# A causal convolution of 31 taps on four engines: the low parts of nine weights by an adding transfer, more taps on GpSimd, TensorE's taps in two chunks

## The chip, the cores and the metric

The kernel runs on one core of a Trainium2 chip. A core has five engines that work side by side, each through its own queue of instructions in a fixed order: TensorE (PE in the profile; PEld is its loading of weights), VectorE (DVE), ScalarE (ACT), GpSimd (POOL) and SyncE (SP), which here only starts transfers. Engines wait for each other through semaphores. The metric is the device time of one execution in microseconds (us). Before the change the median of three runs is 1430.38 us, from 1429.72 to 1431.05.

## The reference

The program is a decoder trunk of two layers over 512 positions of width 1024, in float32. Each layer has a token mixer, a cross-attention into 256 memory tokens and a gated MLP. The change lies in the mixer of the second layer:

```python
def conformer_conv(x, norm, w1, b1, dw_w, dw_b, ln_g, ln_b, w2, b2):
    h = rms_norm(x, norm) @ w1 + b1
    h = jax.nn.glu(h, axis=-1)               # first half times sigmoid(second half)
    h = causal_dwconv(h, dw_w, dw_b)         # 31 taps along the positions, one weight per channel
    h = jax.nn.silu(layer_norm(h, ln_g, ln_b))
    return h @ w2 + b2
...
    m = rms_norm(mem, mem_norm)              # cross-attention, right behind it
    k = (m @ wk).reshape(Bn, M, XA_HEADS, XA_HD)
    v = (m @ wv).reshape(Bn, M, XA_HEADS, XA_HD)
```

The keys and values of the cross-attention depend on the memory alone, so their products can be done at any time before.

## The kernel before

Activations are held transposed: channels on the 128 partitions, in eight chunks of 128, and the 512 positions along the free dimension. TensorE multiplies in a rounded float32 format, so each operand is split into a high part (a rounded copy, made by ScalarE) and a low part (operand minus high part, a subtraction on VectorE or GpSimd). One product of float32 accuracy is then three matmuls (`mm3`, lines 184 to 188): high by high, high by low, low by high. A 128 x 1024 weight has eight 128 x 128 blocks, so one projection onto a chunk (`project`) is 24 matmuls over 512 positions. A key piece (`Memory.products`) is 24 matmuls over 256 memory tokens.

In the conformer (line 1398 on) chunk c goes through these steps. Two projections give its halves, G (the gate) and V. `sigmoid(c)` on ScalarE turns G into the gate; `gated(c)` on VectorE (L1413) multiplies V by it and gives the convolution's input h. The 31 taps of a chunk are shared out:

- `PE_GROUPS[c]` groups of four taps go to TensorE (`conv_pe`, L1443). For them `gated` has GpSimd zero four leading columns of h (L1412) and SyncE start four transfers that stack shifted copies of h (L1420); `taps_of` has GpSimd build the table of tap weights (L1433). A group is four small matmuls, eight records in the profile.
- `N_POOL[c]` taps are set aside (`set_aside`): ScalarE scales a shifted h (L1465, L1468), and GpSimd adds it to a sum (L1469), all but the first.
- The rest are on VectorE (`conv`, L1478 and L1480): one multiply-add each into a bank of PSUM. Two auxiliary banks serve these sums.

`merge(c)` (L1484, VectorE) adds the two sums and the bias. Then follow the sums over channels for the LayerNorm, `quarters` (L298, TensorE): the first half takes chunks 0 to 3, the second half all the rest. TensorE fills the time of the LayerNorm with the products of the memory's values (`Memory.sums`, L458).

Weights stream through three raw buffers and four pairs of high and low buffers. `fetch` starts the transfer of a weight; `weights` splits one that has come. The order is G0, V0, G1, V1, ... G7, V7, then the keys' weights K4 to K7, then the values' R0 to R7. A pair of buffers is given back by the projection that used it, so the split of a weight waits for the projection four places before. The first four splits have their subtraction on VectorE, the later ones on GpSimd (L167 in the profile, as all splits). The weights of keys 0 to 3 have been split and parked by the stage before. Keys 0 and 1 are made before the conformer's projections, key 2 around the first of them.

From the first projection to the last merge the order on all five queues is written out by hand, as a script of steps: G, V project; g is the sigmoid, S the gated product (with the zeroing and the stacking transfers), T a tap on VectorE, P a tap set aside, M a merge, F a fetch and a split, C TensorE's taps, W their table, K a key's products, k and l its high and low part, Q the first half of the channel sums. Each step puts its instructions on its engines' queues, and no queue passes over one that waits. Ahead of the script, where the tokens' scales are computed, a scheduler orders the instructions by priority.

Of the kernel before, what the change touches and what calls it, by code (L numbers as in the profile page):

```python
# [15 lines left out]
P = 128  # L16
# [17 lines left out]
C_RG = 8.0  # L34
TAPS = 31

PE_GROUPS = [0, 0, 0, 4, 0, 0, 4, 6]
N_POOL = [6] * 7 + [5]

KE = 2  # L40
PARKED = 4
# [20 lines left out]
def trunk(ctx: ExitStack, tc: tile.TileContext, I: dict, out: list):  # L62
# [16 lines left out]
    def nm(s):  # L79
        uid[0] += 1  # L80
        return f"{s}_{uid[0]}"
# [1316 lines left out]
    def conformer(norm, nxt, mem, parked):  # L1398
        fold = small.tile([P, 32], F32, tag="fold", name="fold", bufs=1)
        V.tensor_reduce(fold, ident.rearrange("p (a b) -> p a b", b=4), axis=mybir.AxisListType.X, op=ALU.add)  # L1400
        hs, outs = [None] * C, []

        b, psa = [None] * C, [None] * C

# [77 lines left out]

        def merge(c):
            V.scalar_tensor_tensor(zs[c], accs[c], col("c_dw_b", c), zs[c], op0=ALU.add, op1=ALU.add)  # L1484
            outs.append(zs[c])

        def warm(name, func, ins):
            with tc.issue_after(ins):
# [2 lines left out]
        taps, accs, zs, aside, convs = [[None] * C for _ in range(5)]  # L1491
        names = [k + str(c) for c in range(C) for k in "GV"]
        names += ["K%d" % n for n in range(PARKED, C)] + ["R%d" % n for n in range(READY)]
        raws, ws = [], {}

        def fetch():
            if len(raws) < len(names):
                k, n = names[len(raws)][0], int(names[len(raws)][1:])
                src = I["pw1"][n + (C if k == "G" else 0)] if k in "GV" else I["wk" if k == "K" else "wv"][mem.layer * C + n]
                raws.append(wp.tile([P, D], F32, tag="raw", name=nm("raw"), bufs=3))  # L1500
                Memory.fetched = nc.sync.dma_start(raws[-1], src)

        def weights(eng=None):
            k = names[len(ws)]
            ws[k] = load_w(raw=raws[len(ws)], eng=eng, park=k in ("R0", "R1", "R2", "R3"))

        for _ in range(4):
            fetch()
# [3 lines left out]
        warm("token", AF.Sqrt, norm.square)  # L1512
        for n in range(KE):
            mem.keys(n, parked[n])
            if n == 1:
                with tc.high_priority(URGENT):
                    norm.scale()
# [8 lines left out]
        xs = [None] * C  # L1526
        mem.eng = G
        with tc.manual_schedule(engines=ORDERED | {mybir.EngineType.SP}):
            key2 = mem.products(parked[2], ks=range(4))
            ps0 = project_all([ws["G0"], ws["V0"]], norm.x[:1], last=False)  # L1530
            mem.products(parked[2], key2, range(4, C))
            project_all([ws["G0"], ws["V0"]], norm.x[1:], ps0, 1)
            mu = stat_ps()

            def run(script):
                for step in script.split():
                    k, c, n = step[0], int(step[1:2] or 0), int(step[2:] or 1)
                    if k in "GV":
                        raw[step] = project(ws[step], c, norm.x)
                    elif k == "g":  # L1540
                        sigmoid(c, raw["G%d" % c])
                    elif k == "S":
                        psa[c] = raw["V%d" % c]
                        gated(c)
                    elif k == "T":
                        convs[c] = convs[c] or conv(c)
                        for _ in range(n):
                            next(convs[c])
                    elif k == "P":
                        for _ in range(n):  # L1550
                            next(aside[c])
                    elif k == "M":
                        assert next(convs[c] or conv(c), True) and next(aside[c], True)
                        merge(c)
                    elif k == "F":
                        fetch()
                        weights(G)
                    elif k == "C":
                        conv_pe(c)
                    elif k == "W":  # L1560
                        taps_of(c)
                    elif k == "K":
                        raw[step] = mem.products(ws.get(step, parked[c] if c < PARKED else None))
                    elif k == "k":
                        raw[step] = high(raw["K%d" % c][:, :M], mem.key(c)[0])
                    elif k == "l":
                        low(raw["K%d" % c][:, :M], *mem.key(c))
                    elif k == "Q":
                        quarters(mu, outs, c)

            raw = {"V0": ps0[1], "K2": key2}
            sigmoid(0, ps0[0])
            run("k2 l2 G1 F S0 T0 F T0 P0 T0 P0 T0 P0 T02 V1 g1 T0 F T02 P02 T04 G2 F T0 P0 S1 T0 P1 T1 P1 T0 P1 T1")
            run("T0 T1 K3 F T0 T1 g2 T0 P1 T1 V2 T0 P1 T1 k3 l3 T0 T1 T0 T1 P1 T0 T1 G3 F T0 S2 T1 P2 T0 P2 T1 P2 M0")
            run("T2 P2 T1 V3 F T2 T1 g3 T2 P2 T1 P2 T2 T1 T2 T1 T2 G4 F S3 T1 P3 W3 T2 P3 T1 P3 T2 T1 T2 T1 V4 F T2")
            run("g4 T1 P3 T2 P3 T1 T2 T1 T2 T1 G5 F T2 S4 P3 T1 P4 T2 P4 M1 P4 T4 T2 T4 V5 F T2 T4 g5 T2 P4 T4 P4 T2")
            run("T4 T2 T4 T2 C3 F S5 P4 T4 P5 T2 P5 T4 P5 T2 T4 G6 T2 T3 T2 T3 P5 M2 T4 P5 T3 T4 V6 F T3 g6 T4 P5 T3")
            run("T4 T3 T4 T3 T4 G7 F T3 S6 W6 T4 P6 T3 P6 T4 P6 M3 T5 P6 T4 V7 F T5 T4 g7 T5 P6 T4 P6 T5 T4 T5 T4 T5")
            run("K4 F S7 W7 T4 P7 T5 P7 T4 P7 C6 T5 k4 l4 T4 T5 M4 P7 T5 Q0 T5 P7 T6 K5 T5 T6 T5 F T6 K6 T5 F T6 T5")
            run("k5 l5 T6 C7 T5 k6 l6 T6 F T5 T6 F T5 T6 T5 T6 K7 T5 T7 T5 F T7 F T52 k7 l7 T52 M5 M6 F M7 F")  # L1580
            ready = [ws["R%d" % n] for n in range(READY)]
            ps = [[mm_ps(), mm_ps()] for _ in range(2)]
            mem.eng = None
            steps = (_ for h in range(2) for _ in mem.sums(h, ps[h], ready[4 * h :]))

            def go(n):
                for _ in range(n):
                    next(steps, None)

            go(4)  # L1590
            quarters(mu, outs, 1)
            f = split(mu)
            go(1)
            mean, var, sqs = spread(f, fourths), aux_ps(), []
            for c in range(C):
                V.tensor_tensor(outs[c], outs[c], mean, op=ALU.subtract)
                sqs.append(tmp_f())
                A.activation(sqs[c], outs[c], AF.Square)
                if c == 3:
                    go(3)  # L1600
                    quarters(var, sqs, 0)
            raws = []
            for n in range(2):
                raws.append(wp.tile([P, D], F32, tag="raw", name=nm("raw"), bufs=3))
                nc.sync.dma_start(raws[n], I["pw2"][PAIRED[n]])

            def halves(raw):
                both = [split(raw[:, i : i + T]) for i in (0, T)]
                return [b[0] for b in both], [b[1] for b in both]

            pw = [halves(raws[0])]
            go(1)
            quarters(var, sqs, 1)
            f = tmp_f()
            A.activation(f, var, AF.Copy)
            A.activation(small.tile([P, 1], F32, tag="warm", name="root2", bufs=1), sqs[7][:, :1], AF.Sqrt)
            go(1)
            root = stat_ps()
            for j in range(4):
                PE.matmul(root[:, j : j + 1], f[:, j * P : (j + 1) * P], fourth, start=True, stop=True)  # L1620
            rt = small.tile([P, 4], F32, tag="rtok", name=nm("rtok"), bufs=2)
            A.activation(rt, root[:, :4], AF.Sqrt, bias=eps)
            A.activation(small.tile([P, 1], F32, tag="warm", name="silu", bufs=1), eps, AF.Silu)
            V.reciprocal(rt, rt)
            d = diagonals(rt)
            pw.append(halves(raws[1]))
            go(2)
            r = spread(d)
            go(8)

            def scaled(c):
                if c < C:
                    V.tensor_tensor(outs[c], outs[c], r, op=ALU.mult)

            def silu(c):
                if c < C:
                    A.activation(outs[c], outs[c], AF.Silu, scale=col("c_ln_g", c), bias=col("c_ln_b", c))

            scaled(0)
            silu(0)  # L1640
            scaled(1)
            for c in range(C):
                hi = high(outs[c])
                silu(c + 1)
                scaled(c + 2)
                xs[c] = low(outs[c], hi)
                if c == 0:
                    mem.scaled(0, ps[0])
                elif c == 1:
                    pw.append(load_w(I["pw2"][PAIRED[2]]))  # L1650
                elif c == 5:
                    mem.scaled(1, ps[1])
            mem.eng = None
# [212 lines left out]
```

## Time and profile before

| | |
|---|---|
| median of 3 runs | 1430.38 us |
| the profiled execution | 1431.02 us |
| its span, first to last instruction | 1429.2 us |
| mean granted TensorE clock | 0.998 |
| busy: PE / PEld / DVE / ACT / POOL | 99 / 88 / 83 / 56 / 22% of the span |
| transfers | 202.23 MB, mean 141 GB/s |

The conformer takes roughly 740 to 900 us of the span. A row of a timeline gives the start in us, the duration in us, the engine, the line, the operation, output and input, their sizes, and how many equal instructions in a row are merged (x4). In brackets stands how long the engine stood idle just before, and what ended that. Matmuls overlap, so the distance between their starts says more than the duration of one. "DMA to landing" is the time from a transfer's issue to its end.

### The profile page before, as it was taken

The numbers are of one execution on the slowest core, as the hardware profiler recorded it, in microseconds if no ns is written. First come the engines' busy times: TensorE is split into PE (matmuls) and PEld (weight loads), VectorE is DVE, ScalarE is ACT, GpSimd is POOL, SyncE is SP. The second block draws the span as 40 slices with busy tenths as digits, with TensorE's granted clock in tenths as the row PEclk, the third lists the DMA queues.
The fourth block names the chain that finished last, engine by engine and source line by source line (L and its number), as shares of the span: only waits on it lengthen the run. The fifth ranks groups of instructions, "written<-read, shape, count | busy, mean of one in ns | idle before, by whom it ended". The sixth has DMA issues, their size and how long they took to land.

```text
span 1429.2 us, 22885 instructions
## 1 busy us (share of the span) xinstructions
PE 1418.0 (99%) x8578; PEld 1259.4 (88%) x8578; DVE 1184.4 (83%) x1980; ACT 800.7 (56%) x1336; POOL 311.2 (22%) x325
## 2 busy tenths in 40 slices
PE   9999999999999999999999999999999999999998
PEld 7988888998899999999988777899889999999997
DVE  6987776778888888888888997978788988888885
ACT  7678754666644444544555547767665444444434
POOL 0011310200122221222008992010012222221201
PEclk9999999999999999999999999999999999999999
DMA  8523232542577777777432454345247876877741
GB/s 302 197 74 104 89 119 80 118 111 89 136 183 169 172 181 165 164 176 169 140 119 89 118 158 153 105 87 148 86 114 162 178 184 157 171 183 159 164 127 60
DMA packets 78591, 202.23 MB, mean 141 GB/s; under 512 B 8848, under 2 KB 9360, under 8 KB 78480
## 3 DMA queue, kind: packets, MB, share of 16 engines
q1 hardware_dynamic: 50544, 150.15, 33.6%
q0 software_dynamic: 27648, 50.34, 21.3%
q8 instruction: 67, 1.10, 0.3%
q14 instruction: 44, 0.36, 0.1%
q10 hardware_dynamic: 288, 0.27, 0.1%
HBM read 145.16 MB, written 2.10 MB: 103 GB/s over the span
## 4 chain that ended last, share of the span: by engine, by line
PE 90%; DVE 3%; DMA 2%; POOL 2%; issue 1%; ACT 1%; SPq 0%; POOLq 0%; DVEq 0%; ACTq 0%
PE mm L187 22%; PE mm L186 22%; PE mm L188 22%; PE aux L186 7%; PE aux L187 7%; PE aux L188 7%; PE mm L458 2%; DMA raw<-in_wv 1%; DVE wlo L167 1%; POOL actf L1469 1%; ACT whi L166 1%; PE aux L531 0%; POOL act L167 0%; POOL tmp L1290 0%; DMA raw<-in_pw 0%
## 5 line engine op out<-in xcount | busy, mean ns | idle before, releaser
L187 PE MATMUL mm<-act,whi 128*128 128x512 f32 (+2 forms) x1077 | 377.1, 350 | 0.6 <-DVE act L181 0.5
L188 PE MATMUL mm<-act,wlo 128*128 128x512 f32 (+2 forms) x1077 | 376.7, 350 | 0.0
L186 PE MATMUL mm<-act,whi 128*128 128x512 f32 (+2 forms) x1077 | 376.6, 351 | 0.0
L187 PEld LDWEIGHTS mm<-act,whi 128*128 128x128 f32 x1077 | 203.7, 189 | 29.0 <-DVE act L167 1.0
L186 PEld LDWEIGHTS mm<-act,whi 128*128 128x128 f32 x1077 | 203.4, 189 | 28.4 <-ACT tmp L1468 0.8
L188 PEld LDWEIGHTS mm<-act,wlo 128*128 128x128 f32 x1077 | 203.6, 189 | 25.8
L797 ACT ACTIVATE bigr<-raw 128x512 fp32r<-128x512 f32 x168 | 105.6, 628 | 166.8 <-DMA raw<-wa 70.4
L188 PE MATMUL mm<-bigr,bigr 128*128 128x256 f32 x672 | 190.2, 283 | 0.0
L187 PE MATMUL mm<-bigr,bigr 128*128 128x256 f32 x672 | 190.2, 283 | 0.0
L186 PE MATMUL mm<-bigr,bigr 128*128 128x256 f32 x672 | 190.0, 283 | 0.0
L171 DVE TENSOR_TENSOR tmp<-mm,tmp 128x256 f32<-128x256 f32 x336 | 136.3, 419 | 31.6 <-PE mm L188 25.9
L186 PE MATMUL aux<-act,whi 128*128 128x512 f32 x399 | 156.3, 392 | 0.0
L187 PE MATMUL aux<-act,whi 128*128 128x512 f32 x399 | 156.2, 391 | 0.0
L188 PE MATMUL aux<-act,wlo 128*128 128x512 f32 x399 | 155.2, 389 | 0.0
L804 DVE TENSOR_TENSOR bigr<-raw,bigr 128x512 fp32r<-128x512 f32 x168 | 115.5, 688 | 37.0 <-ACT bigr L797 34.8
L166 ACT ACTIVATE whi<-raw 128x1024 fp32r<-128x1024 f32 (+1 forms) x95 | 96.4, 1019 | 84.1 <-PE mm L187 44.0
L187 PEld LDWEIGHTS mm<-bigr,bigr 128*128 128x128 f32 x672 | 128.9, 192 | 1.6
L186 PEld LDWEIGHTS mm<-bigr,bigr 128*128 128x128 f32 x672 | 128.9, 192 | 1.5
L188 PEld LDWEIGHTS mm<-bigr,bigr 128*128 128x128 f32 x672 | 128.9, 192 | 0.0
L807 POOL DMA_DIRECT2D raw<-raw x48 | 41.6, 866 | 343.1 <-DVE wlo L804 283.3
L811 POOL DMA_DIRECT2D raw<-wa x48 | 41.5, 864 | 308.3 <-DVE bigr L804 258.5
L167 DVE TENSOR_TENSOR wlo<-raw,whi 128x1024 fp32r<-128x1024 f32 (+1 forms) x75 | 90.5, 1210 | 20.0 <-ACT whi L166 19.8
(351 smaller groups left out, 3026.1 us busy)
## 6 DMA issues: line engine op xcount, KB each, us to landing
raw<-wa POOLq DMA_DIRECT2D x144, 256.0 KB, 4.6
wa<-in_wpair SPq DMA_DIRECT2D x84, 256.0 KB, 3.5
raw<-in_wpair SPq DMA_DIRECT2D x42, 512.0 KB, 5.7
big<-in_wdown SPq DMA_DIRECT2D x42, 512.0 KB, 6.7
raw<-raw POOLq DMA_DIRECT2D x48, 256.0 KB, 7.6
raw<-in_pw SPq DMA_DIRECT2D x24, 512.0 KB, 3.4
raw<-in_win SPq DMA_DIRECT2D x20, 512.0 KB, 3.4
raw<-in_wk SPq DMA_DIRECT2D x16, 512.0 KB, 3.6
```

The costliest lines, as they stand in the source:

```text
L166: A.activation(hi, src, AF.Copy)
L167: fetched[1] = (eng or V).tensor_tensor(lo, src, hi.bitcast(F32), op=ALU.subtract)
L171: V.tensor_tensor(out, a, b, op=ALU.add)
L186: PE.matmul(ps, wh, xh, start=first, stop=False)
L187: PE.matmul(ps, wh, xl, start=False, stop=False)
L188: PE.matmul(ps, wl, xh, start=False, stop=last)
L458: PE.matmul(p, m[j], x, start=k == 0 and j == 0 and x is hi, stop=k == C - 1 and x is lo)
L797: A.activation(self.w[name][0], self.block(name), AF.Copy)
L804: V.tensor_tensor(lo, self.block(name), hi.bitcast(F32), op=ALU.subtract)
L807: G.dma_start(self.r, self.z, accum_op=ALU.add)
L811: G.dma_start(self.r, self.a22, accum_op=ALU.add)
L1469: G.tensor_tensor(z[:, s:], z[:, s:], f[:, s:], op=ALU.add)
```

## The change

Five things change, all in the conformer.

1. Nine weights (G3, V3, G4, V4, G5, V5, G6, V6, G7) get their low parts in another way: ScalarE writes the high part, then the same copy with a factor of -1 into the low buffer, and GpSimd starts a transfer that reads the weight from memory a second time and adds it there. The subtraction on GpSimd is gone for these.
2. TensorE's taps lie in chunks 6 (6 groups) and 7 (7 groups), where they lay in chunks 3 (4), 6 (4) and 7 (6).
3. The taps set aside become 8 for chunks 0 to 5, 5 for chunk 6 and 3 for chunk 7, where they were 6 for seven chunks and 5 for the last. So GpSimd adds 48 where it added 39, and VectorE has 140 taps where it had 145.
4. Key 3's products come in three pieces in an auxiliary bank: two of the eight blocks between keys 0 and 1, two just before key 2, and the other four in the script's K3.
5. The script is a new one, with another order of all steps. Key 2's copies come after the first gated product. Chunk 7's table (W7) comes early, keys 5 and 4 around chunk 6's taps, keys 7 and 6 before chunk 7's, and the copies of keys 6 and 7 at the end. The last merge is that of chunk 5.

```diff
-PE_GROUPS = [0, 0, 0, 4, 0, 0, 4, 6]
-N_POOL = [6] * 7 + [5]
+PE_GROUPS = [0] * 6 + [6, 7]
+ADDED = ("G3", "V3", "G4", "V4", "G5", "V5", "G6", "V6", "G7")
+N_POOL = [8] * 6 + [5, 3]
...
+                sources[names[len(raws)]] = src
...
         def weights(eng=None):
-            k = names[len(ws)]
-            ws[k] = load_w(raw=raws[len(ws)], eng=eng, park=k in ("R0", "R1", "R2", "R3"))
+            k, raw = names[len(ws)], raws[len(ws)]
+            if k not in ADDED:
+                ws[k] = load_w(raw=raw, eng=eng, park=k in ("R0", "R1", "R2", "R3"))
+                return
+            hi, lo = ws[k] = [wp.tile([P, D], F32R, tag=t, name=nm(t)) for t in ("whi", "wlo")]
+            A.activation(hi, raw, AF.Copy)
+            A.activation(lo, raw, AF.Copy, scale=-1.0)
+            G.dma_start(lo, sources[k], accum_op=ALU.add)
...
             mem.keys(n, parked[n])
+            if n == 0:
+                key3 = mem.products(parked[3], aux_ps(), range(2))
...
+            mem.products(parked[3], key3, range(2, 4))
             key2 = mem.products(parked[2], ks=range(4))
...
-                        raw[step] = mem.products(ws.get(step, parked[c] if c < PARKED else None))
+                        raw[step] = mem.products(*((parked[3], key3, range(4, C)) if c == 3 else (ws[step],)))
...
-            run("k2 l2 G1 F S0 T0 F T0 P0 T0 P0 T0 P0 T02 V1 g1 T0 F T02 P02 T04 G2 F T0 P0 S1 T0 P1 T1 P1 T0 P1 T1")
-            run("T0 T1 K3 F T0 T1 g2 T0 P1 T1 V2 T0 P1 T1 k3 l3 T0 T1 T0 T1 P1 T0 T1 G3 F T0 S2 T1 P2 T0 P2 T1 P2 M0")
...
-            run("T4 T3 T4 T3 T4 G7 F T3 S6 W6 T4 P6 T3 P6 T4 P6 M3 T5 P6 T4 V7 F T5 T4 g7 T5 P6 T4 P6 T5 T4 T5 T4 T5")
-            run("K4 F S7 W7 T4 P7 T5 P7 T4 P7 C6 T5 k4 l4 T4 T5 M4 P7 T5 Q0 T5 P7 T6 K5 T5 T6 T5 F T6 K6 T5 F T6 T5")
-            run("k5 l5 T6 C7 T5 k6 l6 T6 F T5 T6 F T5 T6 T5 T6 K7 T5 T7 T5 F T7 F T52 k7 l7 T52 M5 M6 F M7 F")
+            run("F S0 T0 k2 T04 K3 G1 P02 T0 F T0 P0 F T0 V1 l2 k3 T0 P0 T02 g1 T02 W7 P0 l3 T0 S1 T1 G2 V2 P0 F T0")
+            run("P1 P02 T1 g2 T0 T1 G3 T0 T1 T0 T1 T0 T1 T0 P1 T1 P1 T0 T1 T0 T1 F S2 P12 T1 T0 M0 T1 F P2 T2 P22 P1")
+            run("T1 P1 F T2 V3 g3 P1 T1 P2 T2 T1 P2 T2 F T1 T2 T1 S3 G4 T1 T2 P32 T1 T2 T1 T2 T1 V4 T2 T1 T2 T1 P2 P3")
+            run("T2 T1 M1 F T3 P3 T2 T3 T2 g4 T3 S4 T2 P2 T3 T2 T3 G5 P3 T2 T3 P2 F P3 P4 T2 T3 P4 T2 V5 T3 T2 T3 P4")
+            run("F P4 g5 P3 G6 S5 P4 T3 T2 P3 T3 P4 V6 P5 T2 T32 P4 T2 T3 T2 W6 g6 T3 M2 P5 T3 T4 F T3 P4 T4 P5 T3 F")
+            run("T4 P5 T3 T4 G7 V7 T3 F S6 T4 T3 T4 K5 T3 T4 T3 T4 M3 P5 T5 T4 T5 P6 C6 g7 T4 F T5 K4 F T4 T5 T4 T5")
+            run("k5 l5 P6 T5 T4 T5 S7 P6 T5 F F T4 T5 T4 T5 K7 T4 T5 T4 T5 T4 F P6 T5 P7 K6 T6 P6 T5 T4 T5 k4 T4 T5 F")
+            run("T6 F P5 T5 P7 l4 T5 T4 T5 P5 C7 k6 P7 k7 M6 P5 T5 T4 F T5 T4 T5 Q0 M4 F F M7 T5 M5 l6 l7")
```

In a step such as T02 the first digit is the chunk and the second the number of repeats.

More of the change, by code (lines that the diff above doesn't have):

```diff
@@ L1400, in conformer @@
         V.tensor_reduce(fold, ident.rearrange("p (a b) -> p a b", b=4), axis=mybir.AxisListType.X, op=ALU.add)
-        hs, outs = [None] * C, []
+        hs, outs = [None] * C, [None] * C
         b, psa = [None] * C, [None] * C
@@ L1484, in merge @@
             V.scalar_tensor_tensor(zs[c], accs[c], col("c_dw_b", c), zs[c], op0=ALU.add, op1=ALU.add)
-            outs.append(zs[c])
+            outs[c] = zs[c]
         def warm(name, func, ins):
@@ L1493, in conformer @@
         names += ["K%d" % n for n in range(PARKED, C)] + ["R%d" % n for n in range(READY)]
-        raws, ws = [], {}
+        raws, ws, sources = [], {}, {}
         def fetch():
@@ L1572, in conformer @@
             sigmoid(0, ps0[0])
-            run("k2 l2 G1 F S0 T0 F T0 P0 T0 P0 T0 P0 T02 V1 g1 T0 F T02 P02 T04 G2 F T0 P0 S1 T0 P1 T1 P1 T0 P1 T1")
-            run("T0 T1 K3 F T0 T1 g2 T0 P1 T1 V2 T0 P1 T1 k3 l3 T0 T1 T0 T1 P1 T0 T1 G3 F T0 S2 T1 P2 T0 P2 T1 P2 M0")
-            run("T2 P2 T1 V3 F T2 T1 g3 T2 P2 T1 P2 T2 T1 T2 T1 T2 G4 F S3 T1 P3 W3 T2 P3 T1 P3 T2 T1 T2 T1 V4 F T2")
-            run("g4 T1 P3 T2 P3 T1 T2 T1 T2 T1 G5 F T2 S4 P3 T1 P4 T2 P4 M1 P4 T4 T2 T4 V5 F T2 T4 g5 T2 P4 T4 P4 T2")
-            run("T4 T2 T4 T2 C3 F S5 P4 T4 P5 T2 P5 T4 P5 T2 T4 G6 T2 T3 T2 T3 P5 M2 T4 P5 T3 T4 V6 F T3 g6 T4 P5 T3")
-            run("T4 T3 T4 T3 T4 G7 F T3 S6 W6 T4 P6 T3 P6 T4 P6 M3 T5 P6 T4 V7 F T5 T4 g7 T5 P6 T4 P6 T5 T4 T5 T4 T5")
-            run("K4 F S7 W7 T4 P7 T5 P7 T4 P7 C6 T5 k4 l4 T4 T5 M4 P7 T5 Q0 T5 P7 T6 K5 T5 T6 T5 F T6 K6 T5 F T6 T5")
-            run("k5 l5 T6 C7 T5 k6 l6 T6 F T5 T6 F T5 T6 T5 T6 K7 T5 T7 T5 F T7 F T52 k7 l7 T52 M5 M6 F M7 F")
+            run("F S0 T0 k2 T04 K3 G1 P02 T0 F T0 P0 F T0 V1 l2 k3 T0 P0 T02 g1 T02 W7 P0 l3 T0 S1 T1 G2 V2 P0 F T0")
[6 more added lines that the diff above has]
+            run("T6 F P5 T5 P7 l4 T5 T4 T5 P5 C7 k6 P7 k7 M6 P5 T5 T4 F T5 T4 T5 Q0 M4 F F M7 T5 M5 l6 l7")
             ready = [ws["R%d" % n] for n in range(READY)]
```

## The prediction

> **What bounds the kernel now.** I read the page's first two parts, then the stretch that the diff touches (the conformer's convolution) by windows, the chain of waits through its end, and the timelines of TensorE, VectorE, GpSimd and the SyncE queue there. TensorE is busy 99% of the whole span, so time can only be won where TensorE stands still or has work taken from it.
>
> ```profile
> PE 1418.0 (99%) x8578; PEld 1259.4 (88%) x8578; DVE 1184.4 (83%) x1980; ACT 800.7 (56%) x1336; POOL 311.2 (22%) x325
> ```
>
> Windows over the stretch (columns: span, then busy time and count for PE, PEld, DVE, ACT, POOL; clock; DMA share; GB/s):
>
> ```profile
> 742.00:858.40 116.40, 116.40 (x635) 91.33 (x636) 110.66 (x173) 62.77 (x93) 100.63 (x77) 1.00 0.40 115
> 858.40:864.90 6.50, 5.66 (x28) 4.36 (x26) 4.99 (x8) 2.84 (x4) 5.67 (x4) 1.00 0.65 205
> ```
>
> For 116 us TensorE never stops, at a granted clock of 1.00, while VectorE (95%) and GpSimd (86%, its first work comes at 755.67) are nearly full too. TensorE's few stops lie around that stretch, and these rows of its timeline also give the pace of its work:
>
> ```profile
> 735.30 1.05 PE L314 MATMUL stat<-onesf,tmp 128*128 128x1 f32 x8 [0.80 <-DVE tmp L248]
> ...
> 741.00 0.39 PE L186 MATMUL mm<-act,whi 128*128 128x512 f32 x1
> 741.92 0.50 PE L187 MATMUL mm<-act,whi 128*128 128x512 f32 x1 [0.52 <-DVE act L181]
> ...
> 745.99 0.39 PE L186 MATMUL mm<-act,whi 128*128 128x512 f32 x1
> ...
> 748.71 0.39 PE L186 MATMUL mm<-act,whi 128*128 128x512 f32 x1
> ...
> 836.96 0.28 PE L186 MATMUL mm<-bigr,whi 128*128 128x256 f32 x1
> ...
> 839.72 0.28 PE L188 MATMUL mm<-bigr,wlo 128*128 128x256 f32 x1
> 839.93 3.60 PE L1443 MATMUL mm<-actf,big 128*32 128x512 f32 x32
> 843.34 1.04 PE L298 MATMUL stat<-actf,onesf 128*32 128x512 f32 x8
> ...
> 850.26 5.26 PE L1443 MATMUL mm<-actf,big 128*32 128x512 f32 x48
> 855.45 0.39 PE L186 MATMUL mm<-bigr,whi 128*128 128x256 f32 x1
> ...
> 858.42 5.63 PE L458 MATMUL mm<-act,bigr 128*128 128x512 f32 x24
> 864.89 1.06 PE L298 MATMUL stat<-actf,onesf 128*32 128x512 f32 x8 [0.84 <-DVE actf L1484]
> ```
>
> Twelve wide matmuls take 748.71 - 745.99 = 2.72, so 0.227 each, and a projection (24) 5.44. The 24 narrow ones of a key take 2.88 (0.12 each). Four groups of taps on TensorE cost 3.41 and six 5.19, so two groups are 1.78 and one 0.89. The stops: 0.80 before the token sums at 735.30, 0.69 at 741 (0.92 less one matmul), and 0.84 at 864.89, where the second half of the channel sums waits for the last merge on VectorE. The chain of waits says where that merge was late:
>
> ```profile
> 856.04 3.41 DMA raw<-in_wv
> ...
> 859.48 1.06 ACT whi L166
> 860.54 0.28 ACT bigr L176
> ...
> 863.43 1.41 DVE actf L1484 x2
> ...
> 864.89 1.06 PE stat L298 x8
> ```
>
> A value weight came late, ScalarE's copy of it stood ahead of key 7's copy, and VectorE waited for that.
>
> **The change part by part.** Prices on the other engines, from timelines of VectorE, of GpSimd, and of SyncE's queue:
>
> ```profile
> 755.01 0.74 DVE L1413 SCALAR_TENSOR_TENSOR h<-mm,par,tmp 128x512 f32<-128x512 f32 x1
> ...
> 756.57 10.07 DVE L1478 SCALAR_TENSOR_TENSOR aux<-h,par,aux 128x505 f32<-128x505 f32 x13
> 766.55 0.74 DVE L1413 SCALAR_TENSOR_TENSOR h<-mm,par,tmp 128x512 f32<-128x512 f32 x1
> ...
> 768.50 6.51 DVE L1478 SCALAR_TENSOR_TENSOR aux<-h,par,aux 128x491 f32<-128x491 f32 x10
> 774.92 0.42 DVE L181 TENSOR_TENSOR bigr<-mm,bigr 128x256 fp32r<-128x256 f32 x1
> ...
> 860.84 0.42 DVE L181 TENSOR_TENSOR bigr<-mm,bigr 128x256 fp32r<-128x256 f32 x1 [1.27 <-ACT bigr L176]
> ```
>
> ```profile
> 755.67 4.77 POOL L167 TENSOR_TENSOR wlo<-raw,whi 128x1024 fp32r<-128x1024 f32 x2 [64.56 <-ACT whi L166]
> ...
> 817.72 5.41 POOL L1469 TENSOR_TENSOR actf<-actf,tmp 128x510 f32<-128x510 f32 x4
> 823.09 2.40 POOL L167 TENSOR_TENSOR wlo<-raw,whi 128x1024 fp32r<-128x1024 f32 x1
> ...
> 829.56 0.09 POOL L1412 MEMSET h<- 128x4 f32 x1
> ...
> 841.85 1.49 POOL L1433 TENSOR_TENSOR big<-fold,par 128x768 f32<-128x768 f32 x1
> ...
> 864.08 4.74 POOL L167 TENSOR_TENSOR wlo<-raw,whi 128x1024 fp32r<-128x1024 f32 x2 [0.83 <-ACT whi L166]
> ```
>
> ```profile
> 829.68 4.22 SPq L1420 DMA_DIRECT2D actf<-h  x4
> ...
> 832.20 1.69 SPq L1420 DMA_DIRECT2D actf<-h  x1
> ...
> actf<-h SPq DMA_DIRECT2D x1, 256.0 KB, 5.2
> ```
>
> (The second row is the last of the first row's four; the third is its size and its time to landing.) The adding transfers of another stage, the only ones in this trace:
>
> ```profile
> 449.67 0.86 POOL L811 DMA_DIRECT2D raw<-wa  x1 [7.67 <-DVE bigr L804]
> 450.21 1.21 POOL L809 DMA_DIRECT2D raw<-wa  x1
> ...
> DMA to landing us min/median/max: 3.3/7.6/9.9
> ```
>
> *Key 3 in pieces.* TensorE's work stays the same; six narrow matmuls (0.72) move ahead of key 1, six more to just before the token scale is awaited. They fill the 0.69 stop at 741: gain 0.69. The first projections then end some 0.7 later than at 753.6, but 1.44 of key 3 is already done. On ScalarE and VectorE key 2's copies no longer stand first, so the first gated chunk stays near 755.1.
>
> *TensorE taps in two chunks.* 14 groups become 13: one group at 0.89, and one block fewer with its some 0.1 of switching on each side (855.45 to the next matmul, against 0.12). Gain 1.0. The blocks run later: chunks 6 and 7 only.
>
> *Taps on VectorE.* 145 become 140. A tap that follows one of another chunk costs 0.64 (ten from 768.50 to 774.92), one that follows its own chunk 0.77 (thirteen from 756.57 to 766.55). By the script 12 of the second kind remain of 16. VectorE ran from 755.01 to 864.84 before. It loses 5 x 0.64 + 4 x 0.13 + the 1.27 wait + one key copy of 0.33 that moves behind the merges, 5.3 in all: the last merge ends near 859.6. TensorE gets there, without any stop, at 864.05 - 0.69 - 1.0 = 862.4, so the 0.84 stop goes. These three make 0.69 + 1.0 + 0.84 = 2.5.
>
> *GpSimd's queue.* Nine subtractions at 2.385 (4.77 for two) go, 21.5; nine adds at 1.32 (5.37 for four gives 1.34, narrower ones less) come, 11.9; nine transfers come. They start 0.54 apart, but the first ends at 450.53 and the second at 451.42, so each holds GpSimd 0.88: 7.9. Over the whole queue that is 1.7 less. What counts is the order. Chunk 6's zeroing of the four leading columns (L1412) stands in GpSimd's queue, and its four stacking transfers on SyncE wait for it: 829.56, then 829.68. In the new script stand ahead of it: 5 subtractions (11.9), all nine transfers (7.9), 38 adds (50.2), tap tables of six groups (1.49) and of seven (1.74 by that), small memsets (0.4): 73.6. GpSimd starts at 755.67 + 0.75 (later projections) - 0.26 (key 2's copy gone from ScalarE's head) = 756.2, and loses some 0.5 to ScalarE, whose copies wait for TensorE to give weight buffers back. So the zeroing comes at 830.3 and the last stack lands 832.20 + 5.2 - 829.56 = 7.85 later, at 838.1.
>
> *TensorE at chunk 6.* In its new order stand 14 projections (76.2), half of key 3 (1.44) and key 5 (2.88) before it, 80.5, and 0.9 of switching (before, 85.4 of work took 86.3 from 753.6 to 839.84). From 754.3 it is there at 835.6. It has to wait for 838.1, since the last stack is read first: a new stop of 2.5. Behind it in TensorE's queue stand keys 4, 7 and 6, chunk 7's taps and the sums; none can pass. Its cost is full, because VectorE and GpSimd have slack at the end: the last add of chunk 5 comes before three subtractions, and the queue ended at 868.82 and now ends 1.7 sooner, so that add ends near 868.8 - 1.7 - 7.2 = 860.
>
> One row of ScalarE's timeline, for the scaled taps that feed GpSimd's adds:
>
> ```profile
> 781.11 1.93 ACT L1468 ACTIVATE tmp<-h,par 128x510 f32<-128x510 f32 x3
> ```
>
> *ScalarE* gets nine more copies of 1.06 and nine more scaled taps of 0.64, some 15 us onto 63 of 116: hidden, as long as no copy that waits for a weight buffer holds up a sigmoid; by the order each sigmoid is done 1 us or more before VectorE takes it.
>
> *The nine low parts' landing.* Not shown for 512 KB from memory. A weight's buffer is given back three projections (16.3) before its use; 2.1 for two copies and up to 2 in GpSimd's queue leave 12. Ends: 3.3 as it stands, or 2 x 9.9 = 19.8. I take 8 to 12, between the median and its double but nearer the median, since the stretch's DMA share is only 0.40: hidden.
>
> *The price of a transfer on GpSimd* decides. Ends: 0.54, the distance of the two starts, and 1.73, if it goes with bytes (512 KB against 256). I take 0.88, since both have 128 rows. The Trainium skill's page "DMA: Bandwidth & Descriptors", section "The descriptor swizzle", counts 8 data pairs on each of 16 engines for a transfer of 1 MiB to 128 partitions, one for each row and not for each KB; by that rule the price stays 0.88 and the sum is 0.0, while doubling gives 7.6 more. No run here shows a longer row.
>
> *The sum:* -2.5 + 2.5 = 0.0. The profiled execution took 1431.02 (1429.2 of span and 1.8 around it), 0.64 above the median, so the forecast is 1431.0 for it and 1430.4 as a median.
>
> **The rivals.**
> *Chunk 6 does not wait (faster).* At 0.54 a transfer GpSimd is 9 x 0.34 = 3.1 earlier, the stacks land at 835.0 and the whole 2.5 stays: 1427.9. For it speaks that starts overlap; against, that the second took 1.21.
> *GpSimd late (slower).* Every 0.1 on the price costs 0.9. Above 0.88 the kernel is slower than before, above 1.2 by more than 0.2% (2.9 us, about what a measurement of this kernel tells from no change). At 1.21, the longer row taken whole, it is 3.0 more, 1433.4; at 1.73, 7.6 more, 1438. The longer rows speak for it, the shared 128-row shape against.
> *Low parts late (slower).* Beyond 12 us TensorE waits for the third product of a weight. At 19.8 a weight's round is 8 longer than its room, once for every four weights that share the buffers, so a little over two times: some 17 more, 1447. The DMA load speaks against.
>
> **How the numbers follow.** The forecast (a stop of 0.5 to 4.5 at chunk 6) gets 0.45, no stop 0.25, a late GpSimd 0.23, late low parts 0.07. The case without a stop ends at 1427.9 and in about half of it below 1427.5 (if the 0.80 stop ahead of the token sums is also filled); a late GpSimd is nearly always past 2.9, the forecast's upper edge seldom. Faster 0.14, within 0.2% 0.57, slower 0.29. The range runs from 1427.2 (no stop, with a little more) to 1436.0 (a price of 1.5); the forecast's own is 1428.4 to 1432.4.
>
> **What would show it.** A stop ahead of chunk 6's L1443 block at 835 to 836, ended by the stacking transfers, with the zeroing near 830; the 741 stop gone; none at the second half of the channel sums; nine POOL transfers of 0.88 or so; 13 x 8 L1443 records. Wrong, if GpSimd's transfers are far from 0.88, if they land after 12 us, or if ScalarE starves GpSimd by more than 0.5 before chunk 6.

## The result

The changed kernel takes 1433.78 us (median; 1431.44 to 1436.63) where the kernel before takes 1431.1 beside it on the same chips (1429.72 to 1434.8). The ratio is 1.0015, with a 95% interval of 1.0009 to 1.0021: some 2.1 us slower, real but inside 0.2%. The profiled execution took 1432.95 with a span of 1431.2, 2.0 more than the span before.

**Busy time** hardly moved. The first part of the page after:

```profile
PE 1418.3 (99%) x8570; PEld 1260.9 (88%) x8570; DVE 1180.1 (82%) x1975; ACT 813.9 (57%) x1354; POOL 308.3 (22%) x332
```

TensorE has eight matmul records less, as one group of taps has. What differs is where it stands still, so its timeline is the view that answers:

```profile
735.12 1.05 PE L315 MATMUL stat<-onesf,tmp 128*128 128x1 f32 x8 [0.31 <-DVE tmp L249]
...
835.00 0.28 PE L189 MATMUL mm<-bigr,wlo 128*128 128x256 f32 x1
837.59 5.26 PE L1444 MATMUL mm<-actf,big 128*32 128x512 f32 x48 [2.31 <-DMA actf<-h]
842.78 0.38 PE L187 MATMUL mm<-bigr,whi 128*128 128x256 f32 x1
...
851.60 6.08 PE L1444 MATMUL mm<-actf,big 128*32 128x512 f32 x56
857.49 1.04 PE L299 MATMUL stat<-actf,onesf 128*32 128x512 f32 x8
858.47 5.78 PE L459 MATMUL mm<-act,bigr 128*128 128x512 f32 x24
...
865.51 1.05 PE L299 MATMUL stat<-actf,onesf 128*32 128x512 f32 x4 [1.27 <-DVE actf L1485]
867.00 1.05 PE L299 MATMUL stat<-actf,onesf 128*32 128x512 f32 x4 [0.44 <-DVE actf L1485]
867.98 1.66 PE L459 MATMUL mm<-act,bigr 128*128 128x512 f32 x6
869.47 0.62 PE L351 MATMUL aux<-act,fourths 128*128 128x512 f32 x2
```

The stop at 741 is gone: between 736 and 837 the timeline has no other stop than the foreseen one ahead of chunk 6's taps, which is there (2.31, ended by the stacking transfers). But at the second half of the channel sums, where no stop was expected, there are two. TensorE is there at 865.51 - 1.27 = 864.24 and goes on with the values at 867.98. That is 3.74 for work that takes 0.98 in the first half (857.49 to 858.47), so 2.76 of standing; the brackets show less, since a matmul's duration runs past the next one's start. Against before:

- the stop ahead of the token sums, 0.31 where 0.80 was: -0.49;
- the 741 stop: -0.69;
- taps, 5.19 and 5.89 where three blocks took 3.41 + 5.19 + 3.41: -0.93;
- chunk 6's stop: +2.31;
- the sums' stops, 2.76 where 0.84 was: +1.92.

Together +2.12, and L351 comes at 869.47 where it came at 867.38, +2.09, close to the 2.0 of the whole span. The first of the five can't be put down to the change, though: in the seven traces of kernels that are equal up to the token sums (this one and e1 to e4, e8 and e9 below) that stop reads from 0.31 to 1.07, and traces differ by up to 1.6 in when they get there (734.08 to 735.64). The other four make +2.61. Counted from the start of the token sums to L351 it is 134.35 here and 132.08 before, +2.27; the 0.34 between these two is not placed.

The chain of waits shows what those sums waited for:

```profile
842.90 0.44 SPq L1421
843.44 5.77 DMA raw<-in_wv
...
863.45 1.23 POOL actf L1470
...
864.70 0.75 DVE actf L1485
...
866.19 0.76 DVE actf L1485
867.00 1.05 PE stat L299 x4
```

It leaves TensorE at 842.90, goes through SyncE's queue to the transfer of a value weight, through ScalarE's copy of it, and through GpSimd's adds to the merges of chunks 7 and 5, the last two. The timeline of SyncE's queue says why that transfer started only at 843.44:

```profile
829.76 4.22 SPq L1421 DMA_DIRECT2D actf<-h  x4
834.08 1.28 SPq L1503 DMA_DIRECT2D raw<-in_wv  x2
839.10 4.24 SPq L1421 DMA_DIRECT2D actf<-h  x4
843.44 16.76 SPq L1503 DMA_DIRECT2D raw<-in_wv  x6
```

R2's fetch stands behind chunk 7's four stacking transfers. These wait for chunk 7's gated product until 839.10, and issuing them takes to 843.34. R0 and R1 stand in the same way behind chunk 6's stacks. ScalarE and then GpSimd pay for it, each by its timeline:

```profile
840.21 2.45 ACT L167 ACTIVATE act<-raw 128x512 fp32r<-128x512 f32 x4 [3.33 <-DMA raw<-in_wv]
849.23 1.15 ACT L167 ACTIVATE act<-raw 128x512 fp32r<-128x512 f32 x2 [6.57 <-DMA raw<-in_wv]
```

```profile
770.20 0.87 POOL L1513 DMA_DIRECT2D wlo<-in_pw  x1
770.78 0.41 POOL L1465 MEMSET actf<- 128x1 f32 x1
...
829.63 0.10 POOL L1413 MEMSET h<- 128x4 f32 x1
...
840.91 5.05 POOL L168 TENSOR_TENSOR act<-raw,act 128x512 fp32r<-128x512 f32 x4 [2.02 <-ACT act L167]
849.94 2.54 POOL L168 TENSOR_TENSOR act<-raw,act 128x512 fp32r<-128x512 f32 x2 [3.98 <-ACT act L167]
...
859.80 6.08 POOL L1470 TENSOR_TENSOR actf<-actf,tmp 128x506 f32<-128x506 f32 x5
```

GpSimd stood 2.02 + 3.98 = 6.0 us. The last five adds, behind these splits in its queue, belong to chunks 5 and 7 in turn. Chunk 7's last one ended at 864.68 and let its merge start; a tap and chunk 5's merge follow it on VectorE. Chunk 5's last add ended at 865.88.

### The profile page after: what moved, and what is told of

Its sections match the earlier page's. It is cut to its first block, busy times and chain, and to the rows that moved or that the text cites. A ratio compares the mean times of both kernels' runs of the same rounds, so it can differ in the third digit from the quotient of the medians.

```text
span 1431.2 us, 22883 instructions
## 1 busy us (share of the span) xinstructions
PE 1418.3 (99%) x8570; PEld 1260.9 (88%) x8570; DVE 1180.1 (82%) x1975; ACT 813.9 (57%) x1354; POOL 308.3 (22%) x332
## 3 DMA queue, kind: packets, MB, share of 16 engines
q0 software_dynamic: 28944, 55.06, 23.2%
## 4 chain that ended last, share of the span: by engine, by line
PE 90%; DVE 3%; DMA 3%; ACT 1%; issue 1%; POOL 1%; SPq 0%; ACTq 0%; DVEq 0%; POOLq 0%
PE mm L188 22%; PE mm L189 22%; PE mm L187 22%; PE aux L188 7%; PE aux L187 7%; PE aux L189 7%; DMA raw<-in_wv 1%; PE mm L459 1%; DVE wlo L168 1%; DMA raw<-in_wk 1%; PE aux L532 0%; ACT whi L167 0%; PE mm L1444 0%; DMA actf<-h 0%; POOL tmp L1291 0%
## 5 line engine op out<-in xcount | busy, mean ns | idle before, releaser
L187 PE MATMUL aux<-act,whi 128*128 128x512 f32 x391 | 153.1, 392 | 0.0
L188 PE MATMUL aux<-act,whi 128*128 128x512 f32 x391 | 153.1, 392 | 0.0
L189 PE MATMUL aux<-act,wlo 128*128 128x512 f32 x391 | 152.1, 389 | 0.0
L167 ACT ACTIVATE whi<-raw 128x1024 fp32r<-128x1024 f32 (+1 forms) x86 | 86.9, 1014 | 52.1 <-PE mm L188 15.7
```

Source lines behind the costliest of these rows:

```text
L167: A.activation(hi, src, AF.Copy)
L187: PE.matmul(ps, wh, xh, start=first, stop=False)
L188: PE.matmul(ps, wh, xl, start=False, stop=False)
L189: PE.matmul(ps, wl, xh, start=False, stop=last)
```

## The experiments

Three theories went in. **A**: two waits lie in a row, chunk 6's stacks and the late value weights; TensorE's stop at chunk 6 is covered by the later one, so the end falls only if both go. **B**: the stop at chunk 6 is the whole loss; without it some 2.5 us come back. **C**: the nine adding transfers cost more than they save, through GpSimd's queue or late low parts. All ratios are against the kernel before on the same chip.

### e1: chunk 6's zeroing on VectorE

```diff
             if PE_GROUPS[c]:
-                G.memset(h[:, :4], 0.0)
+                V.memset(h[:, :4], 0.0)
```

> Of the changed kernel one thing is moved: the four leading columns of h in chunks 6 and 7 are zeroed on VectorE (0.06 us each) instead of in GpSimd's queue. Theory A (the loss is set at the end, where the last adds on GpSimd come late because the value weights R0 and R2 come late; R2's fetch stands behind chunk 7's stacks in SyncE's queue): the 2.3 us stop ahead of chunk 6's taps on TensorE goes, the stacks start near 826.5, but R2's fetch stays near 843.4, GpSimd waits for it as before, and the stop before the second half of the channel sums grows from 1.7 to some 4; the time stays within 0.7 us of the changed kernel, some 1433 (1.5 to 2.2 above the kernel before). Rival B (the stop at chunk 6 is the loss): the time falls by its 2.3, to the level of the kernel before.

Measured: 1435.10, ratio 1.0027 (1.0016 to 1.0038). TensorE's timeline of this kernel:

```profile
835.12 5.26 PE L1444 MATMUL mm<-actf,big 128*32 128x512 f32 x48
...
865.30 3.40 PE L299 MATMUL stat<-actf,onesf 128*32 128x512 f32 x8 [3.53 <-DVE actf L1485]
...
871.24 0.62 PE L351 MATMUL aux<-act,fourths 128*128 128x512 f32 x2
```

The stop at chunk 6 is gone and the kernel is no faster, so B falls. The last merge, on VectorE, is as late as it was (865.98 and 0.75 long, against 866.19). TensorE is at the sums 2.47 earlier (865.30 - 3.53 = 861.77, against 864.24) and waits 3.53 for the merges in one piece. That the kernel is even slower was expected by no theory. The same eight records take 3.40 where they take 1.04 in the kernel after, and from the last merge's end to L351 it is 871.24 - 866.73 = 4.51, against 869.47 - 866.95 = 2.52. A window (columns: span, then busy time and count of PE, PEld, DVE, ACT, POOL; clock; DMA share; GB/s) has the reason in the clock column:

```profile
864.50:869.00 4.50, 3.70 (x9) 0.74 (x10) 2.79 (x5) 0.32 (x2) 4.50 (x3) 0.50 0.02 7
```

From within the long stop until about 871 TensorE was granted half its clock. From its coming to the sums to L351 it took 9.47, where the kernel after takes 5.23: 4.24 more, less the 2.47 gained, is 1.77, the difference of the spans (1432.9 and 1431.2).

### e2: R2's fetch ahead of chunk 7's stacks

The step f starts a transfer alone, w does the split alone.

```diff
+                    elif k == "f":
+                        fetch()
+                    elif k == "w":
+                        weights(G)
...
-            run("k5 l5 P6 T5 T4 T5 S7 P6 T5 F F T4 T5 ...")
+            run("k5 l5 P6 T5 T4 T5 f S7 P6 T5 w F T4 T5 ...")
```

> Of the changed kernel one thing is moved: R2's fetch stands ahead of chunk 7's stacking transfers in SyncE's queue, not behind them; R0's split stays where it was. Theory A: R2's fetch starts near 836 instead of 843.4, GpSimd's 4.0 us of idling for it goes, the last add of chunk 5 ends near 862 instead of 865.9, the second half of the channel sums starts when TensorE gets there (864.3), and the kernel wins about 1.7 us: some 1432, within 0.5 of the kernel before. The stop at chunk 6 stays at 2.3. Rival B: the time stays that of the changed kernel, 2 us above the kernel before.

Measured: 1431.85, ratio 1.0009 (1.0000 to 1.0017). TensorE's timeline, then a window behind the stop at chunk 6:

```profile
837.75 6.85 PE L1444 MATMUL mm<-actf,big 128*32 128x512 f32 x48 [2.46 <-DMA actf<-h]
...
865.93 1.07 PE L299 MATMUL stat<-actf,onesf 128*32 128x512 f32 x8
```

```profile
837.70:838.80 1.10, 1.05 (x8) 0.39 (x12) 1.10 (x3) 0.00 (x0) 1.10 (x1) 0.50 1.02 395
```

The late weight was the cause of the stops at the sums: with its fetch moved (R2's transfer is issued at 835.84 instead of 843.44), they are gone. GpSimd's timeline shows the last adds 4.4 earlier (855.35 to 861.44):

```profile
855.35 6.09 POOL L1470 TENSOR_TENSOR actf<-actf,tmp 128x506 f32<-128x506 f32 x5
```

What stays is the stop at chunk 6, 2.46, and half a clock behind it: 48 records in 6.85 instead of 5.26.

### e3: both edits

> Both moves together (zeroing on VectorE, R2's fetch ahead of chunk 7's stacks). Theory A: no stop at chunk 6, none of 4 us on GpSimd, the second half of the channel sums starts near 862, as the prediction's sum without a stop has it: 4 us below the changed kernel, 1.5 to 2.5 below the kernel before (about 1429). Rival B: as with the zeroing alone. Rival C (what is lost is GpSimd's time for the adding transfers or their load on memory): neither move gives more than 1 us, and it stays slower than the kernel before.

Measured: 1429.34, ratio 0.9987 (0.9978 to 0.9995), better than either kernel. TensorE's timeline has no stop left from chunk 6 to the sums:

```profile
835.03 5.26 PE L1444 MATMUL mm<-actf,big 128*32 128x512 f32 x48
...
861.61 1.09 PE L299 MATMUL stat<-actf,onesf 128*32 128x512 f32 x8
...
864.14 0.64 PE L351 MATMUL aux<-act,fourths 128*128 128x512 f32 x2
...
1090.31 0.50 PE L187 MATMUL aux<-act,whi 128*128 128x512 f32 x1 [0.41 <-ACT act L870]
1091.53 0.50 PE L188 MATMUL aux<-act,whi 128*128 128x512 f32 x1 [0.72 <-DVE act L872]
```

The ratios go with A: by itself the first edit adds 0.0012 to the 1.0015 of the change and the second takes 0.0006 away, but together they take 0.0028. The 0.0006 lies within the intervals; that the second edit helps by itself rests on its trace. The last two rows show what became of the gain. L351 came at 867.38 before and comes at 864.14 here, 3.24 earlier, yet the span is only 1.7 shorter (1427.5): 1.13 goes in two stops in the gated MLP, which the kernel before doesn't have, and 0.4 is not placed. Why the operands come no earlier there was not followed up.

### e4: the script without adding transfers

```diff
-ADDED = ("G3", "V3", "G4", "V4", "G5", "V5", "G6", "V6", "G7")
+ADDED = ()
```

> The changed kernel with the nine low parts subtracted on GpSimd again, everything else as changed. A transfer held GpSimd for 0.6 us from its start to the next instruction's, a subtraction 2.38: GpSimd is 9 x 1.8 = 16 us later at chunk 6's zeroing (845 instead of 829.6), TensorE's stop there grows by most of that, and the kernel is 12 to 18 us slower than the changed one: 1446 to 1452. If rival C held and the transfers cost as much as the subtractions, the time would stay near 1434 or fall.

Measured: 1443.63, ratio 1.0093 (1.0078 to 1.0109). The transfers save this kernel some 11 us, so C falls; the size is below the 12 to 18 that were expected, although TensorE has a stop of 4.79 for a late low part that was not expected at all, and half a clock around both stops. TensorE's timeline, then GpSimd's:

```profile
831.46 0.80 PE L189 MATMUL mm<-act,wlo 128*128 128x512 f32 x1 [4.79 <-POOL wlo L168]
...
847.68 6.91 PE L1444 MATMUL mm<-actf,big 128*32 128x512 f32 x48 [4.96 <-DMA actf<-h]
```

```profile
755.12 2.40 POOL L168 TENSOR_TENSOR wlo<-raw,whi 128x1024 fp32r<-128x1024 f32 x1 [64.87 <-ACT whi L167]
...
839.69 0.13 POOL L1413 MEMSET h<- 128x4 f32 x1
```

The zeroing comes 10.06 later than in the kernel after, not 16. GpSimd works without a break from 755.12, 84.57 us; after the change the same queue ran from 755.87 to 829.63 with 1.93 of waiting in between, 71.83 of work. The nine transfers therefore save 12.74 against nine subtractions of 2.35 by their starts, 21.15, which prices one at (21.15 - 12.74) / 9 = 0.93.

### e5 and e6: the kernel before with parts of the change

e5 is the kernel before with the nine adding transfers and its old script. e6 adds key 3 in pieces to it:

```diff
+            if n == 0:
+                key3 = mem.products(parked[3], aux_ps(), range(2))
...
+            mem.products(parked[3], key3, range(2, 4))
...
-            run("k2 l2 ... P0 T02 V1 g1 ...")
-            run("T0 T1 K3 F T0 T1 ... k3 l3 ...")
+            run("k2 l2 ... P0 T02 K3 V1 k3 l3 g1 ...")
+            run("T0 T1 F T0 T1 ...")
```

> The kernel before with one part of the change: the nine low parts (G3 to G7) by the negated copy and the adding transfer; its script, taps and key 3 as they were. Theory A (GpSimd's time and what follows it through raw buffers and SyncE's queue decides): GpSimd is 16 us freer, the value weights come earlier, ScalarE's copy of key 7 is not held up, the last merge ends near 863.5 and the 0.84 us stop before the second half of the channel sums goes: 0.5 to 1.0 us faster than before, about 1430. Rival C (the transfers cost by themselves, by ScalarE's extra copies or load on memory): 1 us slower or more.

> As the kernel before with the nine transfers, and key 3 in pieces too (its last piece and copies moved ahead of V1's, so that the auxiliary bank is free in time). The stop of 0.69 at 741 goes. If TensorE alone is the bound then, 0.5 to 0.7 us faster than with the transfers alone, about 1429.5; if the last merge on VectorE (863.5) sets the end, the same time as with the transfers alone, and a stop of some 0.3 there.

Measured: e5 1430.81, ratio 0.9998 (0.9989 to 1.0006); e6 1430.55, ratio 0.9996 (0.9988 to 1.0005). Neither differs from the kernel before. Neither forecast for e5 came: A's gain of 0.5 to 1.0 did not (VectorE still stood 1.10 for key 7's copy, 1.27 before, and the stop at the sums is 0.67 for 0.84), nor C's loss of 1. The waits of GpSimd in e5 (total, times, longest) say where the saved subtractions went:

```profile
POOL wlo L1513 <- ACT wlo L1512: 11.4, 8, 3.2
```

The old script paces GpSimd by ScalarE's copies, which come when TensorE gives buffers back; the freed time became waiting, 11.4 us. So the transfers are worth something only where the script puts work in their place. TensorE's timeline of e5, then of e6:

```profile
735.03 1.05 PE L315 MATMUL stat<-onesf,tmp 128*128 128x1 f32 x8 [0.29 <-DVE tmp L249]
...
741.64 0.50 PE L188 MATMUL mm<-act,whi 128*128 128x512 f32 x1 [0.53 <-DVE act L182]
...
864.46 1.07 PE L299 MATMUL stat<-actf,onesf 128*32 128x512 f32 x8 [0.67 <-DVE actf L1485]
```

```profile
735.33 1.05 PE L315 MATMUL stat<-onesf,tmp 128*128 128x1 f32 x8 [1.16 <-DVE tmp L249]
...
864.46 1.07 PE L299 MATMUL stat<-actf,onesf 128*32 128x512 f32 x8 [1.17 <-DVE actf L1485]
```

In e6 the 741 stop is filled, and though the stop at 735 is longer (1.16 against 0.29), TensorE comes to the sums 0.5 earlier. They start at 864.46 in both all the same: VectorE's last merge sets that time, and the stop there only grows, 0.67 to 1.17. A filled stop is no gain while a later one on the same engine waits for another engine.

### e8: chunk 6's taps behind key 4

e2's move, and TensorE gets key 4 to do before chunk 6's taps; the zeroing stays on GpSimd.

```diff
-            run("... T5 P6 C6 g7 T4 F T5 K4 F T4 ...")
+            run("... T5 P6 g7 T4 F T5 K4 C6 F T4 ...")
```

> Of the changed kernel two things are moved: R2's fetch ahead of chunk 7's stacks, and chunk 6's taps on TensorE behind key 4 instead of ahead of it. The zeroing stays in GpSimd's queue. Theory A: key 4's 2.9 us of matmuls fill the wait for the stacks, TensorE has no stop there and none at the channel sums, and the time is that of both moves together, 1428.5 to 1429.5, faster than the kernel before. If it were the zeroing itself on GpSimd, and not TensorE's standing still, that mattered, it would stay near 1432.

Measured: 1429.38, ratio 0.9987 (0.9978 to 0.9995), the same as e3. On TensorE's timeline chunk 6's taps start without a stop:

```profile
838.61 5.26 PE L1444 MATMUL mm<-actf,big 128*32 128x512 f32 x48
```

So it is the wait that costs, not the engine that does the zeroing: putting 2.9 us of other work in front of it does as well as ending it sooner.

### e9: the change again

> The changed kernel unchanged, beside the others on one chip. 1433 to 1434, 0.1 to 0.2% above the kernel before. With a granted clock of 0.999 where TensorE's stops leave the clock at full, and 0.997 or 0.998 where it falls to half behind a stop: its runs spread over 3 us or more, those of the version with both moves over less.

Measured, unchanged on the chip of e5, e6 and e8: 1433.34, ratio 1.0016 (1.0007 to 1.0024), as forecast. In TensorE's timeline the stop at chunk 6 and what follows differ from the first profile of the same kernel:

```profile
836.60 6.96 PE L1444 MATMUL mm<-actf,big 128*32 128x512 f32 x48 [2.37 <-DMA actf<-h]
...
864.88 1.78 PE L299 MATMUL stat<-actf,onesf 128*32 128x512 f32 x8
...
868.08 0.62 PE L351 MATMUL aux<-act,fourths 128*128 128x512 f32 x2
```

The stop is 0.06 longer than the 2.31 of the first profile, and here the 48 records took 6.96 instead of 5.26. Yet from the start of these taps to L351 it is 31.48 here and 31.88 in the first profile: the 1.7 lost is taken up by the stops at the sums, which shrink from 2.76 to some 0.7 (864.88 to 868.08 is 3.20, where e2, without a stop, takes 2.49). So the half clock behind chunk 6's stop was not on the path either, as A has it, and it doesn't explain why this kernel's times spread from 1431.25 to 1436.97, or why its median lay 0.8 above the profiled execution. That stays open.

The spread is 5.7 us, against 3.6 in e3 and 3.3 in e8, as expected in direction; the kernel before has 3.7 on this chip. The mean clock doesn't sort the times (0.999 stands at 1431.25 and at 1434.91), so that part of the expectation is not borne out.

## Why the prediction was right, and where it was wrong

The call, within 0.2%, was right and the range held the time. The sum wasn't right: it gave 0.0, and 2.1 came. There is luck in both: the call holds with little to spare (0.15%, interval to 0.21), the time lies above the 1428.4 to 1432.4 that the forecast gave itself, and the range reaches to 1436.0 for a price of a transfer, 1.5, that did not come. By its own steps:

- **Key 3 in pieces** (0.69): right; the stop is gone. e6 adds that the step alone gains nothing.
- **Taps in two chunks** (1.0): 0.93.
- **GpSimd's queue, the price of a transfer** (0.88): right in the sum. An issue is busy 0.87, the same as for the 256 KB transfers of the kernel before; the next instruction starts 0.61 behind its start on average, but those that follow run slower, and net it is 0.93 (e4). The Trainium skill's page "DMA: Bandwidth & Descriptors", section "The descriptor swizzle", counts 9 descriptors a side on each of 16 engines, 144, for a transfer of 1 MiB to 128 partitions. The trace agrees for a row twice as long: the queue of GpSimd's transfers moved 27648 packets for the 192 transfers of 256 KB before the change and 28944 for these and the nine of 512 KB after it, 144 each. The zeroing came at 829.63 (830.3 predicted): there was 1.93 of waiting instead of 0.5, made up by less work than the 73.6 counted.
- **TensorE at chunk 6**: there at 835.28 (835.00 and 0.28; 835.6 predicted), the last stack landed at 837.54 (838.1), the stop 2.31 (2.5). Right in place, cause and size.
- **The low parts' landing** (8 to 12 us, room for 12): better. The answer for line 1513:

```profile
L1513 POOL DMA_DIRECT2D wlo<-in_pw x9: 853/873/1148, 763.8 to 807.3; - x9
...
DMA to landing us min/median/max: 5.7/7.4/8.2
```

  7.4 in the median, 8.2 at most: the rival of late low parts had no ground, and no engine waited for these transfers.
- **"VectorE and GpSimd have slack at the end"**, "the last add of chunk 5 comes before three subtractions, ... near 860": **this is the step that failed**. The add ended at 865.88, so the 0.84 stop before the second half of the sums didn't go: it became 2.76, more than the whole error of 2.1. VectorE's half of the step held: it stood 5.12 for GpSimd's add ahead of chunk 7's merge. The prediction counted GpSimd's own instructions and took 0.5 for waits on ScalarE, which held up to the zeroing within 1.5; behind it came 2.02 and 3.98 on the splits of R0 and R2. It followed the stacking transfers through SyncE's queue to the taps, but not what stands behind them in that queue: the fetches of R0, R1 and R2. Its own chain of the kernel before had named a late value weight as what held up the last merge, and it took that wait off without asking when the value weights come in the new order. e2, which moves one of these fetches and nothing else on any engine, brings the adds to 861.44 and the sums' stops to nothing (TensorE came 1.6 later there by the half clock, but the adds ended 4.49 before it), so this cause is shown.
- **"Its cost is full"** (the stop at chunk 6): wrong for the same reason. With the value weight late, the stop was not on the path: e1 takes it away and gains nothing, and in e9 half a clock behind it costs nothing at L351.

Of the rivals none came: chunk 6 waited, GpSimd was in time there, and the low parts landed early. The loss came from a wait that was not on the list.

## What to carry to other kernels

When a chain of waits names a late transfer before a change, ask when that transfer starts in the new order. Follow a queue past the wait that interests you: four stacking transfers that wait for a product hold up every fetch behind them, and the engine that pays may be three steps away (SyncE, ScalarE, GpSimd, VectorE, TensorE here). Two waits in a row hide each other, so test their removal together before calling either harmless; and where a script sets the pace, cheaper instructions buy nothing until the script puts work in the freed time. A wait can be removed where it is made or by putting other work ahead of it; both gave 0.9987 here.

## What the runs showed of the hardware

TensorE's granted clock fell to half at stops of 2.37 us and more. The clock column of narrow windows dates a fall. In e9:

```profile
836.50:837.00 0.50, 0.40 (x4) 0.16 (x8) 0.50 (x2) 0.00 (x0) 0.46 (x3) 0.82 0.90 344
```

A mean of 0.82 is full clock for 0.32 us and half for the rest, so it fell at 836.82; in the same way it came back at 840.23. In e2 it was half from 837.61 to 841.02, in e1 from 864.26 to 871.09, in e4 from 830.58 to 837.41 and from 847.65 to 851.06: 3.41 us each time, or twice that. On TensorE a fall cost 1.6 to 2.0 (48 tap records in 6.85, 6.91 and 6.96 instead of 5.26; in e1 4.51 instead of 2.52).

It isn't the stop's length alone that decides. The stop of 2.31 left the clock full; 2.37 (e9), 2.46 (e2) and 3.53 (e1) did not, and the falls came 2.59, 2.32 and 2.49 after these stops began, so not at a fixed delay. Every trace has one more fall at its end, where TensorE has no work left: at 1427.33 in e9 and 1428.11 in e2. From the first fall to that one it is 590.51 in both, 173 times 3.4133; in e1 (1430.87) it is 566.61, 166 times the same. So the falls fit the edges of windows of 3.413 us that follow each other without regard to the stops. In the first profile of the changed kernel the last fall is at 1426.86. Counted back in such windows, an edge lies at 836.36, inside the stop of 2.31, which it parts into 1.08 and 1.23. In e9 the whole 2.37 lies in one window, 833.41 to 836.82; in e2 2.32 of the stop lie in one, in e1 2.49. That would explain why 0.06 decided. It is worked out from the edges; no run here moved a stop within its window.

The Trainium skill's page "TensorE: Matmul & The Clock Gate", section "What's actually happening", has the half rate come after an idle window of about 3.4 us, and has that window run freely. The traces agree with the half rate and with the window, but the window need not be idle from end to end: 2.32 us of standing in it were enough in e2.
